# The second MLP product in another order: a regular pair of row tiles first, P5 in a bank of its own, and the last squares on ScalarE

## The chip, the cores and the metric

The kernel runs on one core of a Trainium2 chip. The metric is the device time of one execution in microseconds (us). The engines are named as in the profile: PE is TensorE (matrix products), PEld its loading of the stationary operand, DVE is VectorE, ACT is ScalarE, POOL is GpSimd, and SP is SyncE, whose queue issues the transfers from memory.

## The reference

One layer: a retention mixer, then an MLP with a squared ReLU, each on normalised tokens and added to the residual, and a last normalisation. There are T = 256 tokens of D = 2048, and the hidden width of the MLP is 8192. All numbers are float32. The mixer (four input products, rotary positions, eight heads in chunks of 64 tokens, a head norm and an output product) comes first and is not touched.

```python
def rmsnorm(x, g):
    xf = x.astype(F32)
    y = xf * lax.rsqrt(jnp.mean(xf * xf, axis=-1, keepdims=True) + NORM_EPS)
    return (y * g.astype(F32)).astype(x.dtype)

def squared_relu_mlp(h, w_up, w_down):
    return jnp.square(jax.nn.relu(h @ w_up)) @ w_down

        x = x + y        # y: the retention mixer
        x = x + squared_relu_mlp(rmsnorm(x, norm2[layer]), mlp_w_up[layer], mlp_w_down[layer])
    return rmsnorm(x, final_norm)
```

## The kernel before

Every product is made in three matmuls of rounded float32 parts: each operand is split into a high part (a cast on ACT) and a low part (a subtraction on DVE), and high times high, high times low and low times high are added up in a PSUM bank. Weights arrive by transfers that SP issues (`raw`, `sraw`), and each must be cast into `wh` (ACT) and have `wl` made from it (DVE) before PE can use it. There are four `wh` and four `wl` buffers in the MLP, each for two row tiles of 512 columns or one of 1024.

The MLP runs in four quarters `q` of the hidden width. A quarter first makes 2048 hidden columns: four column groups `c`, each in four banks `acc_u` (lines L87 and L88), after which ACT and DVE turn the banks into the split hidden rows `big` (L542 to L547 of the kernel before: copy, add, ReLU times the row scale, square on ACT, cast, low part). `big` is the stationary operand of the second product. `sums` makes sums of hidden blocks for the first six row tiles.

Then comes the second product, the function `seven`, once for each half of the 2048 output columns, so eight times in all. Its 16 row tiles of weights are treated in two ways. Ten row tiles go through `regular(g)`, two at a time: each group `g` of 0 to 4 loads one block, splits it (L64 and L65) and issues 24 matmuls of 512 columns into the four banks `acc[b][c]` (two blocks of tokens b, two blocks of columns c). The other six row tiles are taken as three pairs, in which the 2 by 2 block product of tokens and columns is done by seven products P1 to P7 in the place of eight. The weights of the four blocks are the tiles b11, b12, b22 and b21 (128 x 1536 each, buffers `sraw`, four of them). A product P1 to P7 is a split of one such tile in two pieces (L147 on ACT, L148 on DVE: 1024 and 512 columns) and nine matmuls of 512 columns (L153). Some products use sums of blocks, which DVE makes in place in `sraw` (L194, L200, L204, L207). A product that belongs to several outputs is accumulated in the bank `chain` (`acc_s`), and `sub_out` adds it to the residual `x` or subtracts it (L557); P5 has no such bank in the kernel before: it opens `acc[1][1]` and is added to `x` from that bank while the bank is still being accumulated, so the next matmul into the bank waits for that read. Banks are tiles of 128 x 512 float32 in a ring of eight (`bufs=8`); the second product takes five of them.

The order inside `seven` is the order in which the code is written: P1, P5, r0, P3, r1, P2, P6, r2, P7, r3, P4, r4 (r is a regular group). All engines work through their instructions in program order, except where the scheduler of the framework moves independent ones past one another; the rows of the order below are what it makes.

When a half is done, `add_residual` adds the four banks to `x` (L433). In the last quarter `finish` also squares each 128 x 512 piece with its sum (`sum_squares`, L437, on DVE), multiplies it by the gain (L506), and, when the last column block of a token block is done, makes the scale of the tokens (L445 and L446, L450 on DVE, the root on POOL at L243) and scales four pieces of `x`, two on DVE (L514) and two on ACT (L512), which are then written out (L515). In the last half, `late=4` keeps four row tiles to the end, so that the four banks end one after the other.

Of the kernel before, what the change touches and what calls it, by code (L numbers as in the profile page):

```python
# [11 lines left out]
AF = mybir.ActivationFunctionType  # L12
# [21 lines left out]
def trunk_kernel(ctx: ExitStack, tc: tile.TileContext, io, out):  # L34
# [14 lines left out]
    def bank(name):  # L49
        return ps.tile([P, 512], F32, tag="bank", name=name)  # L50
# [74 lines left out]

    def seven(quads, blocks, xs, sx, sub_out, done, late=0):
        acc = [[bank("acc_d") for _ in range(2)] for _ in range(NB)]
        chain = bank("acc_s")  # L130
        begun = set()
        raws = []

        def load():
            r = mp.tile([P, SP * 512], F32, tag="sraw", name="sraw", bufs=4)
            nc.sync.dma_start(r, quads[len(raws)])
            raws.append(r)
            return r

        def split(r):  # L140
            parts = []
            for p0 in range(0, SP, 2):
                n = min(2, SP - p0) * 512
                wh = wp.tile([P, 1024], F32R, tag="wh", name="wh", bufs=4)
                wl = wp.tile([P, 1024], F32R, tag="wl", name="wl", bufs=4)
                c = r[:, p0 * 512 : p0 * 512 + n]
                nc.scalar.copy(wh[:, :n], c)  # L147
                nc.vector.tensor_sub(wl[:, :n], c, wh[:, :n].bitcast(F32))  # L148
                parts += [(wh[:, o : o + 512], wl[:, o : o + 512]) for o in range(0, n, 512)]
            return parts  # L150

        def mm(to, key, x, w, last):
            nc.tensor.matmul(to, x, w, start=(key not in begun), stop=last, skip_group_check=True)  # L153
            begun.add(key)

        def product(to, key, r, left):
            parts = split(r)
            for p, (wh, wl) in enumerate(parts):
                xh, xl = left(p)
                mm(to, key, xh, wh, False)  # L160
                mm(to, key, xh, wl, False)
                mm(to, key, xl, wh, p == SP - 1)

        def part(k, b):
            return lambda p: (xs[:, 2 * p + k, 0, b * P : (b + 1) * P], xs[:, 2 * p + k, 1, b * P : (b + 1) * P])

        def total(i):
            return lambda p: (sx[:, p, i, 0], sx[:, p, i, 1])

        def add(kt, wh, wl, b, cs, last=False):  # L170
            t = slice(b * P, (b + 1) * P)
            for c in cs:
                n = slice(c * 512, (c + 1) * 512)
                mm(acc[b][c], (b, c), xs[:, kt, 0, t], wh[:, n], False)
                mm(acc[b][c], (b, c), xs[:, kt, 0, t], wl[:, n], False)
            for c in cs:
                n = slice(c * 512, (c + 1) * 512)
                mm(acc[b][c], (b, c), xs[:, kt, 1, t], wh[:, n], last)

        kept = []  # L180

        def regular(g):
            for j, (wh, wl) in enumerate(load_block(blocks[g], 2, 1024)):
                kt = 2 * SP + 2 * g + j
                if kt >= QT - late:
                    kept.append((kt, wh, wl))
                else:
                    for b in range(NB):
                        add(kt, wh, wl, b, range(2), kt == QT - 1)

        b11, b12 = load(), load()
        product(chain, "s", b11, total(0))
        sub_out(0, 0, chain, -1)
        nc.vector.tensor_add(b11, b11, b12)  # L194
        product(acc[1][1], (1, 1), b11, total(1))
        sub_out(0, 1, acc[1][1], 1)
        regular(0)
        b22 = load()
        product(acc[0][1], (0, 1), b22, total(4))
        nc.vector.tensor_add(b12, b12, b22)  # L200
        regular(1)
        b21 = load()
        product(acc[0][0], (0, 0), b21, part(1, 0))
        nc.vector.tensor_add(b22, b22, b11)  # L204
        product(chain, "s", b22, total(2))
        sub_out(0, 1, chain, 1)
        nc.vector.tensor_add(b21, b21, b22)  # L207
        regular(2)
        product(chain, "s", b12, total(3))
        sub_out(1, 0, chain, -1)  # L210
        sub_out(1, 1, chain, 1)
        regular(3)
        product(acc[1][0], (1, 0), b21, part(1, 1))
        regular(4)
        for b in range(NB):
            for c in range(2):
                for i, (kt, wh, wl) in enumerate(kept):
                    add(kt, wh, wl, b, [c], i == len(kept) - 1)
                done(acc, b, c)
# [211 lines left out]
    def add_residual(acc, half, b, c):  # L431
        n = slice(half * 1024 + c * 512, half * 1024 + (c + 1) * 512)
        nc.vector.tensor_add(x[:, b, n], acc[b][c], x[:, b, n])  # L433

    def sum_squares(b, q):
        n = slice(q * 512, (q + 1) * 512)
        nc.vector.tensor_tensor_reduce(  # L437
            out=scr, in0=x[:, b, n], in1=x[:, b, n], scale=1.0, scalar=0.0,
            op0=ALU.mult, op1=ALU.add, accum_out=ss[:, b, q : q + 1],
        )  # L440
# [55 lines left out]

    def finish(acc, b, half, c):
        add_residual(acc, half, b, c)
        sum_squares(b, 2 * half + c)
        if half == 1 and c == 0:  # L500
            partial_sum(b)
        if half == 1 and c == 1:
            token_scale(rs3, b)
        q = 2 * half + c
        n = slice(q * 512, (q + 1) * 512)
        nc.vector.tensor_mul(x[:, b, n], x[:, b, n], fnorm[:, n])  # L506
        if half == 1 and c == 1:
            r = rs3[:, b : b + 1]
            for q in range(4):
                n = slice(q * 512, (q + 1) * 512)  # L510
                if q % 2:
                    nc.scalar.activation(x[:, b, n], x[:, b, n], AF.Copy, scale=r)  # L512
                else:
                    nc.vector.tensor_scalar_mul(x[:, b, n], x[:, b, n], r)  # L514
                nc.sync.dma_start(out[b * P : (b + 1) * P, n], x[:, b, n])  # L515
# [16 lines left out]
    for q in range(4):  # L532
# [20 lines left out]
        for half in range(2):  # L553

            def sub_out(b, c, acc, sign, half=half):
                n = slice(half * 1024 + c * 512, half * 1024 + (c + 1) * 512)
                nc.vector.tensor_tensor(x[:, b, n], x[:, b, n], acc, op=ALU.add if sign > 0 else ALU.subtract)  # L557

            last = q == 3
            seven(  # L560
                io["w_down_s"][q][half], io["w_down_r"][q][half], hs, sx, sub_out,
                (lambda a, b, c, half=half: finish(a, b, half, c)) if last
                else (lambda a, b, c, half=half: add_residual(a, half, b, c)),
                late=4 if last and half == 1 else 0,
            )

# [69 lines left out]
```

## Time and profile before

| | |
|---|---|
| device time, median of 3 runs | 1491.84 us (1491.62 to 1498.69) |
| the profiled execution's own time | 1493.48 us |
| its span in the trace | 1491.3 us |
| mean granted TensorE clock of the span | 0.994 of full speed |
| PE busy | 1459.9 us, 98% of the span, 7096 matmuls |
| DVE busy | 980.6 us, 66% |
| ACT busy | 728.9 us, 49% |

Busy time counts an instruction from its start to its end; matmuls overlap, so that a busy PE need not be at its peak. The chain that ended last is followed back from the last instruction, at each step to what released it. Idle time of an engine is put down to what came last. The second product of the first quarter begins at 853 us of the span, the others at 1030, 1208 and 1385 us or so, and the last half at 1430 us.

### The profile page before, as it was taken

To read this page: it belongs to the slowest core of one execution; us is meant where nothing else is said; L and a number is where in the kernel's file an instruction comes from. 1 tells how busy PE (TensorE), PEld (TensorE's weight loads), DVE (VectorE), ACT (ScalarE), POOL (GpSimd) and SP (SyncE) were. 2 spreads that over 40 slices of the span, in tenths; PEclk is the share of its full clock that TensorE was granted. 3 is DMA by queue.
4 is the path that set the end of the run, shared out by engine and by line. 5 is a ranking of instruction groups with operands and counts; after the bars stand their busy time and mean duration, and the time that the engine had idled before them with its cause. 6 is when DMAs were issued, how large, how long until landed. Compare 5 with 4: busy or idle time off the path is not lost.

```text
span 1491.3 us, 18087 instructions
## 1 busy us (share of the span) xinstructions
PE 1459.9 (98%) x7096; PEld 1218.4 (82%) x7096; DVE 980.6 (66%) x1313; ACT 728.9 (49%) x978; POOL 16.3 (1%) x28
## 2 busy tenths in 40 slices
PE   9999999999999999999999999999999999999986
PEld 7788888888888888888888878887888878888775
DVE  6556565656565656445467689668886678766896
ACT  6444444444444454434346555555545645455543
POOL 0000000000000000000000000000000000000000
PEclk9999999999999999999999999999999999999999
DMA  9555555455555455755545455653575535655531
GB/s 348 197 176 192 170 177 189 170 182 181 174 179 181 176 170 197 305 203 173 194 170 197 142 200 203 217 174 137 198 245 182 194 134 186 249 194 184 188 136 56
DMA packets 43989, 280.44 MB, mean 188 GB/s; under 512 B 5249, under 2 KB 6145, under 8 KB 14209
## 3 DMA queue, kind: packets, MB, share of 16 engines
q1 hardware_dynamic: 43344, 276.15, 52.9%
q0 software_dynamic: 416, 3.15, 0.6%
q8 instruction: 55, 0.90, 0.2%
q14 instruction: 30, 0.24, 0.0%
q10 hardware_dynamic: 144, 0.01, 0.0%
HBM read 277.18 MB, written 2.10 MB: 187 GB/s over the span
## 4 chain that ended last, share of the span: by engine, by line
PE 94%; DVE 3%; ACT 1%; issue 1%; DMA 0%; POOL 0%; SPq 0%; POOLq 0%; ACTq 0%; DVEq 0%
PE acc_d L153 18%; PE acc_u L87 16%; PE acc_qk L87 8%; PE acc_u L88 8%; PE acc_qk L88 4%; PE acc_v L103 4%; PE acc_v L106 4%; PE acc_o L102 4%; PE acc_o L106 4%; PE acc_o L103 4%; PE acc_g L103 4%; PE acc_g L102 4%; PE acc_v L102 4%; PE acc_g L106 4%; PE acc_s L153 3%; PE po L374 1%
## 5 line engine op out<-in xcount | busy, mean ns | idle before, releaser
L65 DVE TENSOR_TENSOR wl<-raw,wh 128x1024 fp32r<-128x1024 f32 x456 | 554.8, 1223 | 444.9 <-ACT wh L64 444.0
L64 ACT CAST wh<-raw 128x1024 fp32r<-128x1024 f32 x456 | 476.7, 1050 | 571.0 <-PE acc_u L87 124.3
L87 PE MATMUL acc_u<-x1s,wh 128*128 128x512 f32 x1024 | 362.2, 397 | 0.0
L88 PE MATMUL acc_u<-x1s,wl 128*128 128x256 f32 x1024 | 287.8, 281 | 0.0
L153 PE MATMUL acc_d<-wh,big 128*128 128x512 f32 x832 | 262.8, 394 | 3.4 <-DVE x L557 3.1
L87 PEld LDWEIGHTS acc_u<-x1s,wh 128*128 128x128 f32 x1024 | 192.5, 188 | 47.4
L88 PEld LDWEIGHTS acc_u<-x1s,wl 128*128 128x128 f32 x1024 | 192.2, 188 | 0.1
L153 PEld LDWEIGHTS acc_d<-wh,big 128*128 128x128 f32 x832 | 157.2, 189 | 40.1 <-DVE x L557 4.9
L87 PE MATMUL acc_qk<-xs,wh 128*128 128x512 f32 x512 | 181.8, 398 | 0.0
L153 PE MATMUL acc_d<-wl,big 128*128 128x512 f32 x416 | 163.8, 398 | 9.4 <-DVE wl L148 6.9
L88 PE MATMUL acc_qk<-xs,wl 128*128 128x256 f32 x512 | 143.4, 281 | 0.0
L147 ACT CAST wh<-sraw 128x1024 fp32r<-128x1024 f32 x112 | 90.0, 833 | 81.0 <-PE acc_d L153 43.9
L87 PEld LDWEIGHTS acc_qk<-xs,wh 128*128 128x128 f32 x512 | 96.2, 188 | 23.3
L148 DVE TENSOR_TENSOR wl<-sraw,wh 128x1024 fp32r<-128x1024 f32 x112 | 103.5, 952 | 17.8 <-ACT wh L147 16.1
L153 PEld LDWEIGHTS acc_d<-wl,big 128*128 128x128 f32 x416 | 78.4, 190 | 30.3 <-DVE wl L148 9.0
L102 PE MATMUL acc_g<-wh,xs 128*128 128x512 f32 x256 | 100.5, 396 | 2.1 <-ACT wh L72 2.1
L103 PE MATMUL acc_v<-wl,xs 128*128 128x512 f32 x256 | 101.1, 395 | 0.7 <-DVE wl L65 0.7
L103 PE MATMUL acc_g<-wl,xs 128*128 128x512 f32 x256 | 101.0, 394 | 0.0
L102 PE MATMUL acc_v<-wh,xs 128*128 128x512 f32 x256 | 100.4, 393 | 0.3 <-ACT wh L64 0.3
L102 PE MATMUL acc_o<-wh,ys 128*128 128x512 f32 x256 | 100.5, 392 | 0.0
L106 PE MATMUL acc_v<-wh,xs 128*128 128x512 f32 x256 | 100.4, 392 | 0.0
L103 PE MATMUL acc_o<-wl,ys 128*128 128x512 f32 x256 | 100.1, 391 | 0.0
(111 smaller groups left out, 1489.2 us busy)
## 6 DMA issues: line engine op xcount, KB each, us to landing
raw<-in_w_up SPq DMA_DIRECT2D x64, 1024.0 KB, 4.9
raw<-in_w_down_r SPq DMA_DIRECT2D x40, 1024.0 KB, 4.9
raw<-in_w_qk SPq DMA_DIRECT2D x32, 1024.0 KB, 4.9
raw<-in_w_v SPq DMA_DIRECT2D x32, 1024.0 KB, 4.9
raw<-in_w_o SPq DMA_DIRECT2D x32, 1024.0 KB, 4.9
raw<-in_w_g SPq DMA_DIRECT2D x28, 1024.0 KB, 4.9
sraw<-in_w_down_s SPq DMA_DIRECT2D x32, 768.0 KB, 4.4
raw<-in_w_g SPq DMA_DIRECT2D x16, 256.0 KB, 6.3
```

The costliest lines, as they stand in the source:

```text
L64: nc.scalar.copy(wh, r)
L65: nc.vector.tensor_sub(wl, r, wh.bitcast(F32))
L87: nc.tensor.matmul(acc, wh[:, c], both, start=(kt == 0), stop=False)
L88: nc.tensor.matmul(acc[:, :T], wl[:, c], xs[:, kt, 0, :], start=False, stop=(kt == KT - 1))
L102: nc.tensor.matmul(accs[b][c], xs[:, kt, 0, t], wh[:, n], start=(kt == 0), stop=False)
L103: nc.tensor.matmul(accs[b][c], xs[:, kt, 0, t], wl[:, n], start=False, stop=False)
L106: nc.tensor.matmul(accs[b][c], xs[:, kt, 1, t], wh[:, n], start=False, stop=(kt == nk - 1))
L147: nc.scalar.copy(wh[:, :n], c)
L148: nc.vector.tensor_sub(wl[:, :n], c, wh[:, :n].bitcast(F32))
L153: nc.tensor.matmul(to, x, w, start=(key not in begun), stop=last, skip_group_check=True)
L374: nc.tensor.matmul(po, s, w, start=(n == 0), stop=(n == len(terms) - 1))
```

## The change

Three things change, all in the second product of the MLP.

- The steps of `seven` become functions, and a string sets their order; a `w` in it issues the loads of b11, b12, b22 and b21, and each `r` is the next regular group. In seven of the eight halves the order is r0, loads, r1, P1, P3, r2, P2, P5, r3, P6, r4, P7, P4. In the last half it is r0, loads, P1, P3, r1, P2, P5, r2, P6, P4, P7, r3, r4; the last two groups are the four kept row tiles, whose matmuls come at the end as before.
- P5 gets a bank `fifth` (`acc_5`) and is added from it to two pieces of `x`, (0,1) and (1,1); before, its second part stayed in `acc[1][1]`. The second product takes six banks of the ring. The sums of weights stand inside the steps: b11 + b12 and b12 + b22 in P5, b22 + b11 in P6, b21 + b22 in P4.
- In the last quarter the squares go from DVE (the reduction at L437) to ACT (an activation with a sum, L524 of the changed kernel), and the multiplication by the gain, which overwrites `x` in place, stands behind it.

```diff
--- before.py
+++ after.py
@@ -125,9 +125,9 @@
 
 
 
-    def seven(quads, blocks, xs, sx, sub_out, done, late=0):
+    def seven(quads, blocks, xs, sx, sub_out, done, order, late=0):
         acc = [[bank("acc_d") for _ in range(2)] for _ in range(NB)]
-        chain = bank("acc_s")
+        chain, fifth = bank("acc_s"), bank("acc_5")
         begun = set()
         raws = []
 
@@ -188,30 +188,53 @@
                     for b in range(NB):
                         add(kt, wh, wl, b, range(2), kt == QT - 1)
 
-        b11, b12 = load(), load()
-        product(chain, "s", b11, total(0))
-        sub_out(0, 0, chain, -1)
-        nc.vector.tensor_add(b11, b11, b12)
-        product(acc[1][1], (1, 1), b11, total(1))
-        sub_out(0, 1, acc[1][1], 1)
-        regular(0)
-        b22 = load()
-        product(acc[0][1], (0, 1), b22, total(4))
-        nc.vector.tensor_add(b12, b12, b22)
-        regular(1)
-        b21 = load()
-        product(acc[0][0], (0, 0), b21, part(1, 0))
-        nc.vector.tensor_add(b22, b22, b11)
-        product(chain, "s", b22, total(2))
-        sub_out(0, 1, chain, 1)
-        nc.vector.tensor_add(b21, b21, b22)
-        regular(2)
-        product(chain, "s", b12, total(3))
-        sub_out(1, 0, chain, -1)
-        sub_out(1, 1, chain, 1)
-        regular(3)
-        product(acc[1][0], (1, 0), b21, part(1, 1))
-        regular(4)
+        def whole():
+            for name in ("b11", "b12", "b22", "b21"):
+                w[name] = load()
+
+        def plus(to, other):
+            nc.vector.tensor_add(w[to], w[to], w[other])
+
+        def p1():
+            product(chain, "s", w["b11"], total(0))
+            sub_out(0, 0, chain, -1)
+
+        def p2():
+            product(acc[0][0], (0, 0), w["b21"], part(1, 0))
+
+        def p3():
+            product(acc[0][1], (0, 1), w["b22"], total(4))
+
+        def p4():
+            plus("b21", "b22")
+            product(acc[1][0], (1, 0), w["b21"], part(1, 1))
+
+        def p5():
+            plus("b11", "b12")
+            product(fifth, "5", w["b11"], total(1))
+            sub_out(0, 1, fifth, 1)
+            sub_out(1, 1, fifth, 1)
+            plus("b12", "b22")
+
+        def p6():
+            plus("b22", "b11")
+            product(chain, "s", w["b22"], total(2))
+            sub_out(0, 1, chain, 1)
+
+        def p7():
+            product(chain, "s", w["b12"], total(3))
+            sub_out(1, 0, chain, -1)
+            sub_out(1, 1, chain, 1)
+
+        w = {}
+        steps = {"w": whole, "1": p1, "2": p2, "3": p3, "4": p4, "5": p5, "6": p6, "7": p7}
+        g = 0
+        for step in order:
+            if step == "r":
+                regular(g)
+                g += 1
+            else:
+                steps[step]()
         for b in range(NB):
             for c in range(2):
                 for i, (kt, wh, wl) in enumerate(kept):
@@ -496,13 +519,13 @@
 
     def finish(acc, b, half, c):
         add_residual(acc, half, b, c)
-        sum_squares(b, 2 * half + c)
+        q = 2 * half + c
+        n = slice(q * 512, (q + 1) * 512)
+        nc.scalar.activation(scr, x[:, b, n], AF.Square, accum_out=ss[:, b, q : q + 1])
         if half == 1 and c == 0:
             partial_sum(b)
         if half == 1 and c == 1:
             token_scale(rs3, b)
-        q = 2 * half + c
-        n = slice(q * 512, (q + 1) * 512)
         nc.vector.tensor_mul(x[:, b, n], x[:, b, n], fnorm[:, n])
         if half == 1 and c == 1:
             r = rs3[:, b : b + 1]
@@ -561,6 +584,7 @@
                 io["w_down_s"][q][half], io["w_down_r"][q][half], hs, sx, sub_out,
                 (lambda a, b, c, half=half: finish(a, b, half, c)) if last
                 else (lambda a, b, c, half=half: add_residual(a, half, b, c)),
+                "rw13r25r647rr" if last and half == 1 else "rwr13r25r6r74",
                 late=4 if last and half == 1 else 0,
             )
```

Below, pieces of the order of the instructions on an engine. The first is VectorE at the first entry into the second product, in the kernel before. `sraw` is a tile of block weights, `acc_u` a bank of the first product, `big` the hidden rows, `acc_s` the bank of P1.

```order
L194 TENSOR_TENSOR sraw<-sraw 128x1536
L200 TENSOR_TENSOR sraw<-sraw 128x1536
L148 TENSOR_TENSOR wl<-sraw,wh 128x1024
L543 TENSOR_TENSOR s<-acc_u,s 128x256 x2
L544 SCALAR_TENSOR_TENSOR t<-s,rsrow_5800 128x256 x2
L543 TENSOR_TENSOR s<-acc_u,s 128x256 x2
L544 SCALAR_TENSOR_TENSOR t<-s,rsrow_5800 128x256 x2
L557 TENSOR_TENSOR x<-x,acc_s 128x512
L547 TENSOR_TENSOR big<-s,big 128x256 x2
L148 TENSOR_TENSOR wl<-sraw,wh 128x512
L547 TENSOR_TENSOR big<-s,big 128x256 x2
L557 TENSOR_TENSOR x<-x,acc_d 128x512
```

The second is VectorE of the changed kernel at the same entry, from the split of P1 (its first two rows) to that of the third regular group.

```order
L148 TENSOR_TENSOR wl<-sraw,wh 128x1024
L570 TENSOR_TENSOR big<-s,big 128x256
L567 SCALAR_TENSOR_TENSOR t<-s,rsrow_5800 128x256
L148 TENSOR_TENSOR wl<-sraw,wh 128x512
L196 TENSOR_TENSOR sraw<-sraw 128x1536
L570 TENSOR_TENSOR big<-s,big 128x256
L196 TENSOR_TENSOR sraw<-sraw 128x1536
L148 TENSOR_TENSOR wl<-sraw,wh 128x1024
L148 TENSOR_TENSOR wl<-sraw,wh 128x512
L196 TENSOR_TENSOR sraw<-sraw 128x1536
L580 TENSOR_TENSOR x<-x,acc_s 128x512
L65 TENSOR_TENSOR wl<-raw,wh 128x1024 x2
```

The second piece of P5's split (`L148`, 128x512) stood behind two sums and most of the work on the last bank of the first product. Now P1 and P3 are split there, with three sums of weights between them and ahead of the third group's `wl`, and no matmul waits for a read of a bank that is being accumulated.

The third and the fourth are PE at the place where the first of these waits stands (P5 into r0, kernel before) and at the entry into the third regular group (changed kernel). `acc_d_6652` to `acc_d_6655` are the four output banks, and each `wh` and `wl` has its number.

```order
L153 MATMUL acc_d_6655<-wh_6684,big_5801 128x512
L153 MATMUL acc_d_6652<-wh_6700,big_5801 128x512
L153 MATMUL acc_d_6653<-wh_6700,big_5801 128x512
L153 MATMUL acc_d_6654<-wh_6700,big_5801 128x512
L153 MATMUL acc_d_6655<-wl_6685,big_5801 128x512
L153 MATMUL acc_d_6655<-wh_6684,big_5801 128x512
L153 MATMUL acc_d_6655<-wh_6700,big_5801 128x512
L153 MATMUL acc_d_6652<-wl_6701,big_5801 128x512
```

```order
L153 MATMUL acc_d_6653<-wh_6756,big_5801 128x512
L153 MATMUL acc_d_6652<-wh_6771,big_5801 128x512
L153 MATMUL acc_d_6653<-wh_6771,big_5801 128x512
L153 MATMUL acc_d_6654<-wh_6771,big_5801 128x512
L153 MATMUL acc_d_6655<-wh_6771,big_5801 128x512
L153 MATMUL acc_d_6652<-wl_6772,big_5801 128x512
L153 MATMUL acc_d_6653<-wl_6772,big_5801 128x512
```

Before, three matmuls of r0 that need only `wh` stand ahead of the one that needs P5's second `wl`; now four stand ahead of the first one that needs `wl` of the third group, and `wl_6772` is the last row of the piece of VectorE.

The fifth and the sixth are VectorE at the passage between the two halves of the last quarter, before and after.

```order
L194 TENSOR_TENSOR sraw<-sraw 128x1536
L433 TENSOR_TENSOR x<-acc_d,x 128x512 x2
L437 ISA scr,ss<-x 128x512
L437 ISA ss 128x1
L433 TENSOR_TENSOR x<-acc_d,x 128x512
L506 TENSOR_TENSOR x<-x,fnorm 128x512
L437 ISA scr,ss<-x 128x512
```

```order
L148 TENSOR_TENSOR wl<-sraw,wh 128x1024
L456 TENSOR_TENSOR x<-acc_d,x 128x512 x2
L148 TENSOR_TENSOR wl<-sraw,wh 128x512
L529 TENSOR_TENSOR x<-x,fnorm 128x512 x2
L580 TENSOR_TENSOR x<-x,acc_s 128x512 x2
L65 TENSOR_TENSOR wl<-raw,wh 128x1024
L456 TENSOR_TENSOR x<-acc_d,x 128x512 x2
L65 TENSOR_TENSOR wl<-raw,wh 128x1024
L529 TENSOR_TENSOR x<-x,fnorm 128x512 x2
```

The squares are gone from VectorE, and the `wl` of the last half's first regular group (`L65`) stand among the ends of the half before, where a sum of weights and the squares stood ahead of P5's split.

## Rows read from the trace of the kernel before

**Rows 1.** The page: the engines' busy time, and the chain that ended last.
```profile
PE 1459.9 (98%) x7096; PEld 1218.4 (82%) x7096; DVE 980.6 (66%) x1313; ACT 728.9 (49%) x978; POOL 16.3 (1%) x28
PE 94%; DVE 3%; ACT 1%; issue 1%; DMA 0%; POOL 0%; SPq 0%; POOLq 0%; ACTq 0%; DVEq 0%
```

**Rows 2.** PE's waits, 840 to 1491 us: us in all, times, longest.
```profile
PE acc_d L153 <- DVE wl L148: 6.9, 5, 3.5
PE acc_d L153 <- DVE x L557: 3.1, 4, 0.8
PE acc_d L153 <- DVE wl L65: 2.5, 4, 0.6
```

**Rows 3.** PE's timeline at the first entry: start, us, instruction, count, idle before and releaser.
```profile
858.64 0.51 PE L153 MATMUL acc_d<-wl,big 128*128 128x512 f32 x1 [0.86 <-DVE wl L148]
...
860.15 0.51 PE L153 MATMUL acc_d<-wh,big 128*128 128x512 f32 x1 [0.78 <-DVE x L557]
861.29 0.73 PE L153 MATMUL acc_d<-wl,big 128*128 128x512 f32 x2 [0.63 <-DVE wl L65]
```

**Rows 4.** DVE's timeline at the same entry.
```profile
849.07 1.76 DVE L194 TENSOR_TENSOR sraw<-sraw 128x1536 f32<-128x1536 f32 x1
...
852.54 1.22 DVE L148 TENSOR_TENSOR wl<-sraw,wh 128x1024 fp32r<-128x1024 f32 x1
...
857.90 0.68 DVE L148 TENSOR_TENSOR wl<-sraw,wh 128x512 fp32r<-128x512 f32 x1
858.50 0.76 DVE L547 TENSOR_TENSOR big<-s,big 128x256 fp32r<-128x256 f32 x2
859.41 0.69 DVE L557 TENSOR_TENSOR x<-x,acc_d 128x512 f32<-128x512 f32 x1 [0.15 <-PE acc_d L153]
```

**Rows 5.** The chain that ended last: start, us, piece.
```profile
877.81 5.49 PE acc_d L153 x24
...
1437.54 19.18 PE acc_d L153 x71
```

**Rows 6.** PE's and DVE's timelines at the entry into the last half.
```profile
1433.10 0.97 PE L153 MATMUL acc_d<-wh,big 128*128 128x512 f32 x3 [0.26 <-ACT wh L64]
1437.54 0.80 PE L153 MATMUL acc_d<-wl,big 128*128 128x512 f32 x1 [3.47 <-DVE wl L148]
...
1436.26 1.22 DVE L148 TENSOR_TENSOR wl<-sraw,wh 128x1024 fp32r<-128x1024 f32 x1
```

**Rows 7.** Windows: stretch, length, PE, PEld, DVE, ACT, POOL busy, PEclk, DMA share, GB/s.
```profile
853.00:863.00 10.00, 7.73 (x32) 5.51 (x31) 9.65 (x19) 7.22 (x16) 0.00 (x0) 1.00 0.00 1
1437.50:1442.00 4.50, 4.46 (x11) 3.50 (x12) 4.50 (x5) 1.66 (x2) 0.00 (x0) 0.50 0.11 15
```

**Rows 8.** Groups by form: instruction and count, then busy us, mean ns, idle before.
```profile
L147 ACT CAST wh<-sraw 128x1024 fp32r<-128x1024 f32 x56 | 58.8, 1049 | 62.2 <-PE acc_d L153 32.2 <-DVE sraw L194 10.5 <-DVE sraw L204 9.4
L147 ACT CAST wh<-sraw 128x512 fp32r<-128x512 f32 x56 | 34.5, 617 | 18.8 <-PE acc_d L153 11.7 <-PE acc_u L87 7.1
L512 ACT ACTIVATE x<-x,rs 128x512 f32<-128x512 f32 x4 | 2.7, 714 | 11.0 <-POOL rs L243 11.0
L274 ACT ACTIVATION_READ_ACCUMULATOR xh<-xh 128x1 f32 x4 | 0.7, 185 | 0.0
L437 DVE CUSTOM_DVE_ANT_0 scr<-x 128x512 f32<-128x512 f32 x16 | 10.9, 683 | 0.0
```

**Rows 9.** The timeline at the end, all engines.
```profile
1479.20 0.40 PE L153 MATMUL acc_d<-wh,big 128*128 128x512 f32 x1
...
1483.56 0.21 DVE L450 TENSOR_SCALAR ms<-ss,ms 128x1 f32<-128x1 f32 x1
...
1483.86 0.93 POOL L243 TENSOR_TENSOR rs<-ms,mhalf 128x1 f32<-128x1 f32 x1 [3.73 <-DVE ms L450]
1484.82 1.33 ACT L512 ACTIVATE x<-x,rs 128x512 f32<-128x512 f32 x2 [3.32 <-POOL rs L243]
```

**Rows 10.** DMA issues on the page: KB each, us from issue to landing.
```profile
sraw<-in_w_down_s SPq DMA_DIRECT2D x32, 768.0 KB, 4.4
```

## The prediction

> **What bounds the kernel now.** I read the page first. PE is busy for 98% of the span and carries 94% of the chain that ended last; DVE has 3% of it and ACT 1% [rows 1]. So a gain comes from PE's idle time or from the ends of the program, and the change adds and removes no matmul. The second view is PE's list of waits over the four quarters of the MLP [rows 2]: all that PE waits for there is in the second product, and it is DVE's work, bar one wait for ACT. One wait of 3.5 us stands by itself; the rest are 0.85, 0.78 and 0.63 us four times over, once at each entry into the second product.
>
> The third view is the first entry [rows 3, 4]. P1 begins at 853.27. The second piece of P5's `wl` starts on DVE only at 857.90, since DVE first had two sums of weights (1.76 us each) and then the ends of the last column group; PE's first wait, 0.86 us, is for it. Then `sub_out` reads `acc[1][1]` at 859.41, and the next matmul into that bank waits 0.78 us. DVE only then makes the `wl` of r0, and PE waits 0.63 us. DVE was busy for 9.65 of these 10 us [rows 7]: it is late, not idle. The price is 0.86 + 0.78 + 0.63 = 2.27 us in each of four quarters, **9.1 us**.
>
> The fourth view is the last half [rows 5, 6]. PE waits 0.26 us for a cast and 3.47 us for P5's `wl`, which starts at 1436.26, behind a sum and a row of squares, residual adds and gains of the half before. After that wait the granted clock is 0.50, which is 1.2 of 2.4 GHz [rows 7]. What this costs I take from the chain: 24 matmuls take 5.49 us at full clock, 0.2288 us each [rows 5], so that the 71 of the piece from 1437.54 should take 16.24 us; they take 19.18, which is 2.94 more. Together 0.26 + 3.47 + 2.94 = **6.7 us**. The other half boundaries have no wait in [rows 2], so the squares, which only the last quarter has, are what made this one late.
>
> The last view is the end [rows 9]: PE's last matmul ends at 1479.60; the last row scale begins on DVE at 1483.56 (after add, square, partial sum and a gain), POOL takes 0.93 us, and the scaling starts at 1484.82, 5.22 us after PE.
>
> **The change, part by part.** I walk through the order of the changed kernel with t = 0 at the first matmul of the second product, and with durations from start to start when an engine runs on: a sum of weights 1.67 (its row shows 1.76 of busy time), a `wl` of 1024 columns 1.15 (1.22), one of 512 columns 0.60 (0.68), a residual add or `sub_out` 0.60 (0.69) [rows 4], a cast of 512 columns 0.62 [rows 8], a matmul 0.2288 [rows 5].
>
> *Entry.* r0 and r1 are 48 matmuls, 10.98 us, that need only hidden rows and weights of long before. Their four banks in the ring of eight are those of the last column group but one, so nothing is waited for. The ends of the last group lie beside them, where they stood in P5's way. P1 is due at 10.98; its split is done at about 6.9. P3 is due at 13.04, its split is done at 12.5. The critical piece is the third regular group. On DVE, the second piece of P1's split can start at 6.34, because its `wh` buffer is free only when r0's 24th matmul ends (23 x 0.2288 + 0.39 = 5.65) and the cast takes 0.62. Then follow, in the order shown: `wl` and a handoff to 7.06, a sum to 8.73, `big` 0.34 to 9.07, a sum to 10.74, P3's `wl` to 11.89 and 12.60, a sum to 14.27, P1's `sub_out` to 14.87, and the group's `wl` to 16.09. PE reaches the group after 48 + 18 matmuls and has four that need `wh` alone, so it asks at 70 x 0.2288 = 16.02. The wait is about 0.1 us. In the second half of a quarter there are no ends of a column group and DVE is a little ahead (57.88 against 57.96). Both are tight: a handoff of 0.03 to 0.05 us more on each of the nine DVE steps makes 0.3 to 0.4 us of wait. I allow 0.2 us per half: 8 x 0.2 = 1.6, and the gain of the seven halves and four entries is 9.1 - 1.4 = **7.7 us** (the last half's 0.2 stands in its own sum).
>
> *P5, P2, P6, P7, P4.* P5's bank has a second `sub_out`, 0.60 us more of DVE per half; a half lasts 42 us and DVE is at 66% [rows 1], and no matmul waits for the read any more, since the fifth bank is not written again in the half. Without that cover it would cost 8 x 0.60 = 4.8 us. The sums in P5, P6 and P4 were there before, each with its 1.67 us; all come at least one regular group (5.49 us) ahead of their product, except P4's in the last half. The boundary between halves is tight too: P7's two `sub_out`s and the next half's first `wl` end at 42.52, PE asks at 42.63.
>
> *Transfers.* The four tiles of weights are asked for together, after r0's block; each can start when the last split from its buffer is done, by the same walk at about 22 (b11), 29, 35 and 39 us (b21) into the half before, and lands 4.4 us later [rows 10]. The half lasts 42 us and P1 comes 11 us into it, so the nearest margin is over 5 us, and the regular blocks behind them on SP's queue are no nearer. I cost this at nothing; one late tile would cost at most its 4.4 us.
>
> *Last half.* DVE's twelve steps of the boundary (four adds, four squares, four gains) become eight; 4 x 0.60 = 2.4 us leave it. Its order keeps one regular group ahead of P1. I find four waits: P1's cast behind two squares on ACT (0.15), the cast of r2 (0.4), P4 (1.0), and 0.1 at the entry. P4's comes about like this: from P5's end DVE still has 0.7 us of r2's `wl`, two `sub_out`s (1.2), the sum of P6 and directly behind it that of P4 with a partial sum between (3.7 with handoffs); P4's cast, 1.05, is done at 6.7, and PE, after r2's 24 matmuls and one of P6, asks at 5.7. Together 1.7 us in the place of 6.7: **5.0 us**. None is as long as the 3.47 that the clock followed.
>
> *Squares on ACT, end.* A square of 128 x 512 with its sum has no row. The bounds: the cast of 512 columns, 617 ns, from below, and the scaling of 512 columns plus the read of a sum, 714 + 185 = 899 ns, from above; on DVE it is 683 [rows 8]. I take 0.81, nearer the upper end, because L512 is an activation as this one is. At the end both engines share the chain: the last add starts 0.88 after PE's end (it stands behind the gain of the block before it, which waits for that block's square), ends at 1.57, the square at 2.4, the scale's POOL step at 3.67, and the scaling starts at 3.70, against 5.22: 1.5 us. With ends far apart (0.62 to 0.90 twice on the path) it is 1.3 to 1.9; for handoffs I count **1.3 us**.
> One row speaks against it: a scaling of 512 columns takes longer on ACT (714 ns) than the square on DVE (683) [rows 8]. The Trainium skill ("ScalarE: Activation LUTs", Rules for kernel authors) says that products belong on VectorE and not on ScalarE; the trace agrees by these 31 ns, no more. By that rule alone the end would be no shorter, and the sum 1.3 us smaller; by the rows the square leaves an engine that has more behind it.
>
> **The sum.** 7.7 + 5.0 + 1.3 = 14.0 us off the profiled execution's own 1493.48, so 1479.5. That execution is 1.6 us above the median of the runs, 1491.84; off this it is 1477.8, and I take **1478**.
>
> **The rivals.** A difference under 0.5%, 7.5 us, is no change here.
>
> 1. *DVE is late at the third group by a `wl`* (chance 0.10). Without the four matmuls that need only `wh`, or with 0.1 us more per DVE step, the wait is about 1.1 us in all eight halves: 8 x 0.9 = 7.2 more, and the time 1485. For it: margins of 0.1 us, DVE busy 97% of the entry [rows 7]. Against: all durations are of rows, and nine of them have no spread to speak of.
> 2. *Slower: the sums stand in the way of every half* (0.05). Three sums, 1.67 each, now stand between P1's split and the third group's `wl`. If PE waits at P3 as well as at r2, because P1's split comes later by the casts it waits for, each half pays that. The point from which it decides: without the 1.6 us of waits the gain is 15.6 us, which over eight halves is 1.95 us each. At 2.8 us each the time is 1491.84 - 15.6 + 22.4 = 1498.6. Against: it needs half of DVE's 5 us uncovered, and two regular groups, 10.98 us, stand ahead.
> 3. *The clock falls after short waits* (0.07). The last half has four, 1.7 us together. Should the clock be 0.50 after them, 2.94 us come back, once: 1481. Against: after three waits of 2.27 us at the entry the clock stays at 1.00 [rows 3, 7]. The Trainium skill ("TensorE: Matmul & The Clock Gate", A second HAM failure mode: psum-queue depth-cycling) says that short idling between groups of matmuls can make the clock swing; the entries of this trace do not show it.
> 4. *The change does little*: the three waits move to P1 and P3, and only the last half gains (0.05). Then 5.0 + 1.3 = 6.3: 1485.5.
>
> **How the numbers follow.** The forecast has 0.73, with 1475 (no wait at all and the better end: 1491.84 - 9.1 - 6.2 - 1.5) to 1481 as its own range. Rivals 1, 3 and 4 add times up to 1485.5. The range 1474.5 to 1485.5 leaves out about 0.15. Faster by over 0.5% means under 1484.4: the forecast, rival 3, and a share of the two that end near 1485 (0.05): 0.85. Same: the rest of those, 0.10. Slower: rival 2, 0.05.
>
> **What would show it.** Right: no PE wait for L580 at all; none over 0.5 us for L148 or L65 at the four entries; r0 and r1 back to back with the last column group; clock 1.00 from 1430 us on; in the last half one wait near 1 us at P4. The scaling begins 3.5 to 4 us after the last matmul. Wrong: PE waiting for L65's `wl` at the third group in each half by 1 us or more, or for `sraw` sums (L196) at P6 or P4 in the common order; a transfer that lands after its split is due; an ACT square far from 0.8 us.

## The result, and the profile after

The changed kernel takes 1472.85 us (median of 4 runs, 1472.58 to 1474.12) against 1491.84: a ratio of 0.9863, 95% interval 0.9835 to 0.9892. The forecast was 1478 with a range from 1474.5 to 1485.5: the direction and the places were right, and the gain was larger than the range allowed. The profiled execution has a span of 1470.5 us against 1491.3. One execution of the kernel before took 5292 us and is left out of the ratios and ranges.

The page: the engines' busy time and the chain that ended last, which answer to [rows 1].

```profile
PE 1453.9 (99%) x7096; PEld 1215.9 (83%) x7096; DVE 978.7 (67%) x1305; ACT 735.3 (50%) x994; POOL 16.3 (1%) x28
PE 96%; DVE 1%; ACT 1%; issue 1%; DMA 0%; POOL 0%; SPq 0%; POOLq 0%; ACTq 0%; DVEq 0%
```

PE's waits from 840 us on (us in all, times, longest), beside [rows 2]: every wait that was listed at the four entries is gone, and two short ones for ACT are left, both in the last half.

```profile
PE acc_d L153 <- ACT wh L147: 0.5, 1, 0.5
PE acc_d L153 <- ACT wh L64: 0.3, 1, 0.3
```

Windows of the first entry and of the last half (columns as in [rows 7]). PE has 46 matmuls in the first 10 us, where 32 stood before; DVE is nearly as busy as it was (9.31 us of the ten against 9.65); the clock is 1.00 in both.

```profile
850.50:860.50 10.00, 10.00 (x46) 8.23 (x45) 9.31 (x17) 6.87 (x14) 0.00 (x0) 1.00 0.39 139
1434.00:1450.00 16.00, 15.24 (x65) 11.67 (x64) 15.81 (x18) 9.52 (x12) 0.00 (x0) 1.00 0.00 1
```

DVE at the first entry, from P1's second split to the third regular group, and PE's first use of that group's `wl`. The second product begins at 850.53; the first `wl` is done at 865.42 + 1.22 - 850.53 = 16.11 us after it, where the walk had 16.09, and PE uses it at 16.16 without a listed wait, 0.14 us after the 16.02 of the walk: a delay too short to have a row.

```profile
856.88 0.69 DVE L148 TENSOR_TENSOR wl<-sraw,wh 128x512 fp32r<-128x512 f32 x1 [0.42 <-ACT wh L147]
857.61 1.76 DVE L196 TENSOR_TENSOR sraw<-sraw 128x1536 f32<-128x1536 f32 x1
859.28 0.42 DVE L570 TENSOR_TENSOR big<-s,big 128x256 fp32r<-128x256 f32 x1
859.62 1.75 DVE L196 TENSOR_TENSOR sraw<-sraw 128x1536 f32<-128x1536 f32 x1
861.29 1.82 DVE L148 TENSOR_TENSOR wl<-sraw,wh 128x1024 fp32r<-128x1024 f32 x2
863.14 1.76 DVE L196 TENSOR_TENSOR sraw<-sraw 128x1536 f32<-128x1536 f32 x1
864.82 0.68 DVE L580 TENSOR_TENSOR x<-x,acc_s 128x512 f32<-128x512 f32 x1
865.42 2.35 DVE L65 TENSOR_TENSOR wl<-raw,wh 128x1024 fp32r<-128x1024 f32 x2
...
866.69 0.74 PE L153 MATMUL acc_d<-wl,big 128*128 128x512 f32 x2
```

The end. PE's last matmul ends at 1460.59, the last scaling starts at 1464.21: 3.62 us, against 5.22 [rows 9]. A square takes 0.63 and its read of the sum 0.19; they overlap, and from the start of the one to the end of the other it is 0.73.

```profile
1460.20 0.39 PE L153 MATMUL acc_d<-wh,big 128*128 128x512 f32 x1
...
1461.43 0.68 DVE L456 TENSOR_TENSOR x<-acc_d,x 128x512 f32<-128x512 f32 x1
1462.20 0.63 ACT L524 ACTIVATE scr<-x 128x512 f32<-128x512 f32 x1 [1.49 <-DVE x L456]
1462.74 0.19 ACT L524 ACTIVATION_READ_ACCUMULATOR scr<-x 128x1 f32 x1
...
1464.21 1.33 ACT L535 ACTIVATE x<-x,rs 128x512 f32<-128x512 f32 x2 [1.29 <-POOL rs L266]
```

Where the 20.8 us between the two profiled executions lie, from the first matmuls of the stages: 2.74 ahead of the second product (853.27 against 850.53); 2.65 in each of three quarters (532.13 against 524.19 from the first entry to the fourth); 8.33 from the fourth entry to PE's end (94.20 against 85.87); 1.8 from there to the end of the span.

### The profile page after: what moved, and what is told of

Its sections match the earlier page's. It is cut to its first block, busy times and chain, and to the rows that moved or that the text cites. A ratio compares the mean times of both kernels' runs of the same rounds, so it can differ in the third digit from the quotient of the medians.

```text
span 1470.5 us, 18118 instructions
## 1 busy us (share of the span) xinstructions
PE 1453.9 (99%) x7096; PEld 1215.9 (83%) x7096; DVE 978.7 (67%) x1305; ACT 735.3 (50%) x994; POOL 16.3 (1%) x28
## 4 chain that ended last, share of the span: by engine, by line
PE 96%; DVE 1%; ACT 1%; issue 1%; DMA 0%; POOL 0%; SPq 0%; POOLq 0%; ACTq 0%; DVEq 0%
PE acc_d L153 18%; PE acc_u L87 16%; PE acc_qk L87 8%; PE acc_u L88 8%; PE acc_qk L88 4%; PE acc_v L103 4%; PE acc_o L102 4%; PE acc_o L106 4%; PE acc_o L103 4%; PE acc_g L103 4%; PE acc_v L106 4%; PE acc_g L102 4%; PE acc_v L102 4%; PE acc_g L106 4%; PE acc_s L153 3%; PE po L397 1%
## 5 line engine op out<-in xcount | busy, mean ns | idle before, releaser
L65 DVE TENSOR_TENSOR wl<-raw,wh 128x1024 fp32r<-128x1024 f32 x456 | 553.4, 1223 | 429.1 <-ACT wh L64 428.6
L153 PE MATMUL acc_d<-wh,big 128*128 128x512 f32 x784 | 245.2, 392 | 0.8 <-ACT wh L147 0.5
L153 PEld LDWEIGHTS acc_d<-wh,big 128*128 128x128 f32 x784 | 147.2, 188 | 33.9 <-ACT wh L147 0.9
L153 PE MATMUL acc_d<-wl,big 128*128 128x512 f32 x392 | 150.1, 393 | 0.0
L148 DVE TENSOR_TENSOR wl<-sraw,wh 128x1024 fp32r<-128x1024 f32 x112 | 103.3, 952 | 11.9 <-ACT wh L147 11.3
L102 PE MATMUL acc_g<-wh,xs 128*128 128x512 f32 x256 | 100.3, 395 | 1.1 <-ACT wh L72 1.1
L106 PE MATMUL acc_g<-wh,xs 128*128 128x512 f32 x256 | 99.7, 389 | 0.0
```

Source lines behind the costliest of these rows:

```text
L65: nc.vector.tensor_sub(wl, r, wh.bitcast(F32))
L102: nc.tensor.matmul(accs[b][c], xs[:, kt, 0, t], wh[:, n], start=(kt == 0), stop=False)
L106: nc.tensor.matmul(accs[b][c], xs[:, kt, 1, t], wh[:, n], start=False, stop=(kt == nk - 1))
```

## Experiments

Ratios are to runs of the kernel before on the same chip, whose medians in the three sets were 1493.08, 1495.11 and 1493.44 us.

| run | us | ratio, 95% interval |
|---|---|---|
| P5's bank alone | 1501.86 | 1.0050 (1.0032 to 1.0068) |
| squares on ACT alone | 1487.51 | 0.9957 (0.9944 to 0.9971) |
| order and bank, squares on DVE | 1479.94 | 0.9905 (0.9886 to 0.9923) |
| no regular group first | 1484.66 | 0.9939 (0.9926 to 0.9952) |
| one regular group, then P1, P5 | 1476.66 | 0.9887 (0.9872 to 0.9903) |
| one regular group, then P1, P3 | 1474.20 | 0.9862 (0.9840 to 0.9883) |
| the changed kernel again | 1473.07 | 0.9862 (0.9847 to 0.9877) |
| P7 ahead of P4 in the last half | 1475.52 | 0.9869 (0.9849 to 0.9889) |
| gain taken into the scale | 1473.76 | 0.9860 (0.9838 to 0.9881) |
| these last two together | 1474.05 | 0.9864 (0.9842 to 0.9887) |
| one regular group, gain in the scale | 1471.65 | 0.9852 (0.9837 to 0.9867) |

**The kernel before, once more.**

> The kernel before, unchanged, for a second trace. Theory A: 2.74 us of the difference of the two profiled executions lie ahead of the second product (its first matmul at 853.27 before, at 850.53 after), in code that the change doesn't touch, and are a matter of the single execution: the start of the first weights' matmuls (13.91 against 12.66) and a granted clock of 0.66 in 60 to 65 us against 1.00. By A this second execution need not show the clock of 0.66, and its second product starts somewhere between 850.5 and 853.3; the three waits at each entry and the 3.5 us of the last half come again to 0.1 us. Rival: the early loss belongs to the program before, and comes again in full, 853.3 with the clock near 0.66.

Its span is 1490.2 us (1492.3 us in all). The second product begins at 851.13, and the granted clock in 60 to 65 us is 1.00, so the early 0.66 belongs to single executions. Three of the runs below, whose code is the same up to the second product, show it too: 0.66 with P5's bank alone, 0.68 with one regular group, 0.66 with P7 ahead of P4. The waits come again. But now the clock falls behind the first entry's waits, and not behind the second's, which are the same:

```profile
851.00:861.00 10.00, 7.92 (x28) 5.47 (x27) 9.64 (x19) 7.07 (x15) 0.00 (x0) 0.86 0.00 1
...
1029.00:1039.00 10.00, 7.73 (x33) 5.53 (x32) 9.64 (x19) 7.56 (x17) 0.00 (x0) 1.00 0.00 0
```

That quarter lasts 178.48 us and the next two 177.40 each. So the entries had a price that the first trace did not show, paid in some executions: 1.1 us here.

**P5's bank alone.** In the kernel before:

```diff
-        chain = bank("acc_s")
+        chain, fifth = bank("acc_s"), bank("acc_5")
...
-        product(acc[1][1], (1, 1), b11, total(1))
-        sub_out(0, 1, acc[1][1], 1)
+        product(fifth, "5", b11, total(1))
+        sub_out(0, 1, fifth, 1)
+        sub_out(1, 1, fifth, 1)
```

> The kernel before with P5 in a bank of its own and its two sub_outs, the order and the squares as before. Theory A (the entry's waits are one backlog of DVE; the bank read is only one of its three faces): the wait for the sub_out goes, the next one for r0's wl grows by as much and by up to the 0.6 us of the second sub_out; time between 1490 and 1494 us, no gain. Rival B (the read of the bank is a cost of its own): four waits of 0.78 plus about 0.11 of restart each are gone, 3.6 us, 1488 us.

It is slower. PE at the first entry, and two windows: the waits for the read and for r0's `wl` have become one of 2.51 us, which ends 8.63 us after the entry in the place of 8.02, later by the 0.6 of the second `sub_out`; and with it the clock falls at all four entries.

```profile
858.27 0.51 PE L153 MATMUL acc<-wl,big 128*128 128x512 f32 x1 [0.63 <-DVE wl L148]
861.53 1.22 PE L153 MATMUL acc_d<-wl,big 128*128 128x512 f32 x2 [2.51 <-DVE wl L65]
```
```profile
863.00:868.00 5.00, 5.00 (x15) 3.95 (x14) 4.33 (x4) 1.04 (x1) 0.00 (x0) 0.59 0.78 247
...
1043.00:1048.00 5.00, 5.00 (x13) 3.90 (x12) 4.68 (x5) 1.04 (x1) 0.00 (x0) 0.50 0.79 229
```

A quarter lasts 180.5 to 180.8 us. Theory A was right on the wait (it moves and grows) and had not priced the clock; rival B falls.

**The squares on ACT alone.** The kernel before with `finish` as in the changed kernel.

> The kernel before with the last squares on ACT and nothing else. Theory A: 1.6 to 1.8 us come off the end, and with three squares of 0.60 us each gone ahead of P5's wl the wait of 3.5 us in the last half falls to about 1.7; whether the clock still falls after it is open: 1488.5 us if it does, 1485.5 if it doesn't. The entries keep their 2.3 us. Rival C (the squares matter only at the end): 1490.2 us.

The last half's waits are now 1.06 and 0.40 us, the clock stays at 1.00 from 1430 to 1450, and the stretch from the fourth entry to PE's end shrinks from 94.20 to 89.29 us, by 4.9.

```profile
1438.44 0.50 PE L153 MATMUL acc_d<-wl,big 128*128 128x512 f32 x1 [1.06 <-DVE wl L148]
1439.58 0.73 PE L153 MATMUL acc_d<-wl,big 128*128 128x512 f32 x2 [0.40 <-DVE wl L65]
```
```profile
1430.00:1450.00 20.00, 18.54 (x80) 14.58 (x79) 19.93 (x23) 11.22 (x18) 0.00 (x0) 1.00 0.31 108
```

From PE's last matmul (1477.17) to the scaling (1480.66) it is 3.49 us. So C falls. The clock did not fall in the last half, for which A has 1485.5; the median is 2.0 us over it. The runs scatter from 1484.2 to 1491.4, since the entries' waits are still there and the clock behind them is not always the same: the profiled execution (1489.13 us) has quarters of 177.38, 180.05 and 178.87 us, with a clock of 1.00, 0.85 and 0.89 in the ten us of their entries. The two shortest runs, 1484.2 and 1484.5 us, have a mean granted clock of 0.998, the longest one 0.994.

**Order and bank, squares back on DVE.**

> The changed kernel with the last squares back on DVE: the order and the fifth bank alone. Theory A (the order pays at the four entries, 2.65 us each, and in the last half only together with the squares): 1.7 us are lost at the end and the last half's boundary waits 1 to 2.4 us more for DVE; 1475.5 to 1477 us, 1480 if the clock falls as well. Rival C (the squares matter only at the end): 1474.5 us, with the last half's waits as in the changed kernel.

The entries are as in the changed kernel (quarters of 174.7 us). In the last half DVE's four squares and three of the gains come ahead of r0's `wl`, and the wait is longer than the 3.47 us before the change, with the clock at half after it:

```profile
1423.66 1.22 PE L153 MATMUL acc_d<-wl,big 128*128 128x512 f32 x2 [4.14 <-DVE wl L65]
```
```profile
1423.00:1428.00 5.00, 4.34 (x10) 3.47 (x11) 5.00 (x7) 0.52 (x1) 0.00 (x0) 0.50 0.31 79
```

From the fourth entry to PE's end it is 91.76 us against 85.87. From PE's last matmul (1467.82) to the scaling (1471.73) it is 3.91 us against 3.62, so the squares are worth 0.3 us there, not the 1.7 expected: each of the two, the order or the squares, takes most of the old 5.22 away by itself. The last add shows it: it started 1.97 us after PE's end before (the first row), and starts 0.66 us after it here (the second), 0.72 with the squares alone and 0.84 with both.

```profile
1481.57 0.69 DVE L433 TENSOR_TENSOR x<-acc_d,x 128x512 f32<-128x512 f32 x1
```
```profile
1468.48 0.69 DVE L456 TENSOR_TENSOR x<-acc_d,x 128x512 f32<-128x512 f32 x1
```

No run has the new order without the fifth bank, so what the bank is worth in it is not shown.

**One regular group in the place of two.** The common order as `"rw13r25r6r7r4"`.

> The changed kernel with one regular group ahead of P1 and P3 in the place of two, in the seven halves of the common order (r0, loads, P1, P3, r1, P2, P5, r2, P6, r3, P7, r4, P4). Theory A (two groups, 10.98 us of matmuls, are the cover for DVE's backlog at the entry): one group covers 5.49, P1's split is ready at 6.9 by the walk and P3's later, so PE waits 2 to 4 us at each of the four entries and the granted clock falls after it in some or all of them, for 1 to 2.5 us each: 1483 to 1495 us. Rival D (the fifth bank and the place of the sums do it, the second group is not needed): 1473 us.

PE has no wait at all from 845 us to the fourth entry, and the second product of the first quarter takes 936.42 - 852.23 = 84.19 us against 84.29 with two groups. Theory A falls, rival D stands: the second group is not needed. DVE's rows show how: between P1's and P3's splits and the `wl` of the next group (L65, 8.4 us after the entry) there is one sum of weights now, in the place of three, so the order of the sums changed with the order of the steps.

```profile
857.75 1.75 DVE L196 TENSOR_TENSOR sraw<-sraw 128x1536 f32<-128x1536 f32 x1
859.42 0.68 DVE L148 TENSOR_TENSOR wl<-sraw,wh 128x512 fp32r<-128x512 f32 x1
860.02 0.68 DVE L580 TENSOR_TENSOR x<-x,acc_s 128x512 f32<-128x512 f32 x1
860.62 2.35 DVE L65 TENSOR_TENSOR wl<-raw,wh 128x1024 fp32r<-128x1024 f32 x2
```

**No regular group at the opening.** `"w13r25r6r7r4r"`.

> The changed kernel with no regular group ahead of P1 and P3 in the seven halves of the common order (loads, P1, P3, r0, P2, P5, r1, P6, r2, P7, r3, P4, r4); P5 in its own bank and not at the opening. Theory E (a regular group at the opening is needed, one is enough): P3's second piece of wl is behind the ends of the last column group as P5's was, PE waits 0.5 to 1 us there and again at r0, 1.5 to 2.5 us in each of four entries with the restarts, and the clock may fall: 1479 to 1487 us. Rival F (only P5 at the opening was the trouble, because its sum and its bank come early): no wait, 1473 us.

The waits are there again, two in the place of three, for P3's second `wl` and for r0's, and the granted clock is 0.87 to 0.89 in the first 10 us of three of the four entries.

```profile
856.48 0.51 PE L153 MATMUL acc_d<-wl,big 128*128 128x512 f32 x1 [0.82 <-DVE wl L148]
858.29 1.19 PE L153 MATMUL acc_d<-wl,big 128*128 128x512 f32 x2 [0.84 <-DVE wl L65]
```

11.6 us over the changed kernel of the same call. E holds, F falls: the regular group at the opening is needed even when P5 comes late.

**One regular group, then P1 and P5 as before.** `"rw15r3r26r7r4"`.

> The changed kernel with one regular group at the opening and then P1 and P5 as before the change (r0, loads, P1, P5, r1, P3, r2, P2, P6, r3, P7, r4, P4). Theory G (both are needed: a regular group first, and no sum of weights between P1's split and the next product): P5's split stands behind two sums, P1's sub_out and the ends; by the DVE rows of the run with one group its wl is done about 10.7 us after the entry, PE asks at 7.6 and waits 3 us, and the clock falls: 1487 to 1497 us. Rival E (a regular group first is all that is needed): 1474 us.

3.6 us over the changed kernel, not 14 or more. P5's `wl` is not waited for by name: PE starts P5 (`acc`), goes on with four matmuls of the next group, after 0.79 us of waiting for that group's cast, and returns to P5. The clock stays at 1.00.

```profile
858.37 0.39 PE L153 MATMUL acc<-wh,big 128*128 128x512 f32 x1
859.54 1.20 PE L153 MATMUL acc_d<-wh,big 128*128 128x512 f32 x4 [0.79 <-ACT wh L64]
860.58 0.39 PE L153 MATMUL acc<-wl,big 128*128 128x512 f32 x1
```

From 858.37 to 860.58 there are 5 matmuls, 1.14 us, so 1.07 are lost. The quarters last 175.4 to 176.2 us against 174.6 with P3 in P5's place. So the regular group first does most of the work, and P5's late place the rest; G's 3 us of waiting left out that PE takes matmuls of the next group ahead of P5's.

**P7 ahead of P4 in the last half.** `"rw13r25r674rr"`.

> The changed kernel with P7 ahead of P4 in the last half. Theory A: P4's sum then has P7's nine matmuls (2.06 us) more cover, and the wait of 0.50 us for P4's cast with its restart is gone: 0.5 to 1.0 us, 1472.1 us. Rival: the wait moves to the kept groups, whose casts come later: 1472.9 us, no difference.

No gain: P4's wait stays (0.44) and P7 gets one (0.48 for its `wl`). From the fourth entry to PE's end it is 86.63 us, 0.8 more. The sum was not the only thing late. That two products which follow each other directly have no cover for their splits is my reading, and not tested: P4 and P7 follow each other in the changed kernel too, and there P7 has no listed wait.

**The gain taken into the scale.** `finish` leaves out the gain of one column block, and the scaling of that block does both:

```diff
-        nc.vector.tensor_mul(x[:, b, n], x[:, b, n], fnorm[:, n])
+        if not (half == 1 and c == 0):
+            nc.vector.tensor_mul(x[:, b, n], x[:, b, n], fnorm[:, n])
...
+                elif q == 2:
+                    nc.vector.scalar_tensor_tensor(x[:, b, n], x[:, b, n], r, fnorm[:, n], op0=ALU.mult, op1=ALU.mult)
```

> The changed kernel with the gain of the third column block of the output taken into the row scale (one operation on DVE), so that the last residual add doesn't stand behind that gain and the square before it. Theory A (the end is DVE's and ACT's chain from the last matmul; the last add starts 0.84 us after it for that reason): 0.8 us off the distance from the last matmul to the scaling (3.62 us to 2.8): 1472.0 us. Rival: the end is set by the transfers of the results, 6.3 us from the scaling to the end of the span, and the wider operation on DVE gives it back: 1472.9 us.

The last add still starts 0.50 us after PE's end, since the small addition of the partial sum (L469) is ahead of it and waits for the same square. From PE's last matmul to the scaling it is 3.27 us: 0.35 less, not 0.8, and too little for this run to tell from nothing.

> Both of these edits together, the version that should beat both kernels. Theory A: 1.3 to 1.8 us under the changed kernel, 1471.3 us. If only one of the two helps, its share alone.

With P7's order the two make 1474.05 us, no gain.

**The changed kernel again, and the best version.**

> The changed kernel, unchanged, as the measure for the other three on the same chip: 1472.6 to 1474.1 us, the second product of a quarter 84.3 us from its first matmul to the next product's, no wait at the entries.

> One regular group at the opening, and the gain of the third column block taken into the row scale: the two edits that shortened their own stretch by the traces (second product 84.2 against 84.3 us in each quarter and 85.6 against 85.9 in the last; last matmul to scaling 3.3 against 3.6 us). If they add up: 0.9 us under the changed kernel in the same call. Rival: both are inside the scatter, no difference.

Against the changed kernel on the same chip (1472.66 to 1473.60) the runs lie at 1471.56 to 1471.80: 1.4 us less, and the two sets do not touch. That is more than the 0.9 expected. The last add now starts 0.03 us after PE's last matmul, which ends at 1460.42, and the scaling at 2.83 us, where the same edit alone had 3.27: DVE's order has come out otherwise, with the small addition (L469, at 1461.06) behind the last add.

```profile
1460.45 0.69 DVE L456 TENSOR_TENSOR x<-acc_d,x 128x512 f32<-128x512 f32 x1 [0.24 <-PE acc_d L153]
...
1463.25 1.33 ACT L536 ACTIVATE x<-x,rs 128x512 f32<-128x512 f32 x2 [1.29 <-POOL rs L266]
```

## Why the prediction was right in direction and wrong in size

- **The bound and the places: right.** DVE's backlog at the four entries, the late `wl` of the last half with the clock behind it, and the end are where the time came off, and no wait for `sub_out` is left.
- **Entry: the walk was right, the price of a wait was not.** This is the step that failed: "The price is 0.86 + 0.78 + 0.63 = 2.27 us in each of four quarters". The second product of the first quarter took 940.19 - 853.27 = 86.92 us before and takes 84.29; its 366 matmuls at 0.2288 us would take 83.74. So the entry cost about 3.1 us and not 2.27. The idle time in a row counts from the end of the matmul before, which lies 0.16 us after the start that a next one would have had (0.39 - 0.2288), and the matmul after a wait takes 0.51 in the place of 0.39 [rows 3]: 0.27 per wait, 0.8 per entry. Two other runs agree where their clock was 1.00. Without a regular group first, the second quarter's product takes 86.00 us, 2.26 over its matmuls, and its two waits are 0.82 + 0.83 + 2 x 0.27 = 2.19. With P1 and P5 as before, one wait of 0.79 lost 1.07, and 0.79 + 0.27 is 1.06. What the walk leaves over, 0.4 us a quarter, was measured at 0.55. The gain is 2.63 us a quarter where 1.9 was forecast: four times 0.73, **2.9 of the 5.2 us** between forecast and median. The range had the same fault: its end of 1475 takes off every wait, but at 2.27 us an entry.
- **Last half: right in its places, 0.7 us short.** From the fourth entry to PE's end 8.33 us came off; without the entry's 2.63 that is 5.7 against 5.0. The 6.7 us for the kernel before left out the same 0.27 behind its two waits, of which about 0.1 is in the 2.94 already: that explains 0.4. Of the four waits forecast, two have rows, 0.26 and 0.50; P4's cast ends, as worked out, after its sum directly behind that of P6, but half as late as I had it. The runs with one part alone show that here it is the squares that count: 4.9 us with them alone, nothing with the order alone (its 2.44 is the entry's).
- **The end: a right number, half by luck.** The square and its read take 0.73 us from start to end, against the 0.81 taken. From PE's last matmul to the scaling 1.60 us came off, where the walk had 1.5 and I counted 1.3 for handoffs that were not lost; 0.2 more lies behind the scaling: 1.8 in all, 0.5 over the forecast. But I had put all of this down to the squares, and the order and the bank bring 1.31 of it without them (5.22 to 3.91); in the changed kernel the squares are worth 0.3 there.
- **Rivals.** The third group's `wl` was due within 0.1 us, as worked out, and PE lists no wait for it, so rival 1 and rival 2 fall at the walk's own margin. The waits did not move to P1 and P3; rival 4 falls too. The clock does not fall in the changed kernel; rival 3 was wrong of the kernel after but right of the kernel before. I held against it that the clock stayed at 1.00 behind 2.27 us of waits; the second trace of before shows 0.86 behind the same waits. The Trainium skill ("TensorE: Matmul & The Clock Gate", A second HAM failure mode: psum-queue depth-cycling) speaks of a clock that swings with short idling between groups of matmuls; the traces of the kernels with these three waits agree, with 1.00 at some entries and 0.85 to 0.89 at others.
- **What stays open:** the remaining 1 us or so between the forecast from the median and the result. It is hardly the clock behind the entries. Each trace of the kernel before has one short fall of the clock ahead of the last half, and a mean granted clock of 0.994; of the 38 executions of that kernel with a clock on record, those at 0.995 took 1491.1 to 1492.2 us, those at 0.994 took 1492.3 to 1495.1, and the slowest, at 0.988, 1499.9. So its scatter goes with the clock, and the median of 1491.84 lies, by its time, among the runs without such a fall. The changed kernel's eight runs, all at 0.998, took 1472.6 to 1474.1. In the traces of all these kernels the second product begins between 850.5 and 853.3 us, after code that no run changed, and in the two of the changed kernel it is earliest. The rest may lie there; that is argued, not shown.

## What to carry to other kernels

A wait in a row of idle time costs more than the row says: compare the length of the whole stage with its matmuls at full rate, and take the difference as the price. Where a stage begins with work that depends on a busy engine, open it with matmuls whose operands are long ready; 5.5 us of them were enough here, and the second group brought nothing. Removing one of several waits on the same backlog moves it on, and was slower than leaving it, since the merged wait was longer and the clock fell with it at every entry.

## What the runs showed of the hardware

The same three waits, 2.27 us in all, were followed by a granted clock of 1.00 at four entries of one execution, and by 0.86 in the first ten us of one entry (a mean of 1.00 and 0.50, the two levels in the traces) and 1.00 at the other three in another execution of the same program. One wait of 2.51 us behind one of 0.63 was followed at all four entries by 0.50 to 0.86 in the 5 us after the first ten. Where the three waits were followed by a fall, it cost the quarter 1.1 us in one trace and 2.7 and 1.5 in another; the waits themselves cost 3.1. The activation with a sum takes 632 ns for 512 columns in the changed kernel's second trace, near the cast's 617 and under the scaling's 714 [rows 8], and the read of its sum 186.
